# Weight-block sums made by accumulating DMAs instead of VectorE, in a seven-product matrix scheme with other signs

## The chip, the cores and the metric

The kernel runs on one core of one Trainium2 chip. The metric is the device time of one execution in microseconds, as the median of several runs. The kernel before took 1541.83 us (median of three, 1540.9 to 1542.78).

## The reference

Two layers of an encoder over 512 positions of width 2048, all in float32. Each layer normalises its input, multiplies it by one wide weight (`w_in`, 2048 x 4928), feeds three groups of heads and a gate, and projects back with `w_o` (2048 x 2048):

```python
for l in range(DEPTH):
    h = rmsnorm(x, pre_norm_g[l])
    z = h @ w_in[l]
    q_lat, kv_lat, k_pe, gb, gc, xin, q_mem, gate = split_cols(z)
    ...   # latent attention (8 heads), short gated convolution, attention over 256 memory tokens
    y = jnp.concatenate([a_out, c_out, m_out], axis=-1) * jax.nn.silu(gate)
    o = y @ w_o[l]
    x = x + rmsnorm(o, post_norm_g[l])
```

Only the two large products, `h @ w_in` and `y @ w_o`, are touched by the change.

## The kernel before, in words

**Precision.** A float32 operand is held as two parts that TensorE takes in one pass, `hi` and `lo`. A product is three matmuls, hi·hi, hi·lo and lo·hi (`mm3`, lines 233 to 235). A weight tile is split after it has been loaded: ScalarE makes `wh` (line 161), VectorE then makes `wl` as the difference (line 162).

**Seven products for eight.** The large products are worked out in groups of 1024 output columns (one group has 832). There are seven groups in a layer, five of `w_in` and two of `w_o`, so 14 in all. A group is a 2 x 2 block product, done by a scheme of the Strassen-Winograd kind: seven block products P1 to P7 on sums of blocks instead of eight. The left sums (`S1` to `S4`) are made once for a matrix by `combine` and split. The right sums are sums of weight blocks and are made for each group: T1 = B12 - B11, T2 = B22 - T1, T4 = B21 - T2 and T3 = B22 - B12. Before the change VectorE makes them out of loaded tiles (`sub`, line 408) into tiles of a pool `tf` (3 buffers), and they are split from there.

**Units and steps.** The depth of 1024 of a block is cut into four chunks, c = 0 to 3. A unit is one chunk of one block or sum, a tile of 128 x 1024 floats (512 KB). A step takes one unit and does 12 matmuls of 512 columns on it (2 row tiles, 2 halves of the chunk, 3 parts). `HEAD`, `STEADY`, `SECOND` and `LATE` list the passes of a group; a pass of several products takes their chunks in turn. `Program.run` walks the steps: before a step it issues loads some units ahead on the queue of SyncE (line 136, pool `raw`, 5 buffers) and emits the splits of units up to two steps ahead (`wh` and `wl` have three buffers each). Work that can wait (left sums, normalisation) is put in a queue and taken out as room allows.

**Order.** The instructions of TensorE and SyncE stand in the order in which the program records them; the others are put in order by a scheduler. VectorE has the splits, the sums, the evictions from PSUM and the softmax. GpSimd (POOL) has little: a few statistics of one column and some DMAs that are not weights.

Of the kernel before, what the change touches and what calls it, by code (L numbers as in the profile page):

```python
# [60 lines left out]
RAW, TF, PIECES, SLABS = 5, 3, 4, 19  # L61


class Unit:
# [4 lines left out]
    def __init__(self, loads, make=None, alloc=None, gain=None, split=True):  # L69
        self.loads = loads  # L70
        self.make = make
        self.alloc = alloc
        self.gain = gain
        self.split = split


class Program:
    def __init__(self, nc, raw, hi, lo, ahead=2, loads_ahead=3):
        self.nc = nc
        self.pools = raw, hi, lo  # L80
        self.ahead, self.loads_ahead = ahead, loads_ahead
        self.steps = []
        self.early = 0
        self.queue = []
# [29 lines left out]
    def run(self):  # L114
# [4 lines left out]
        at = {"load": 0, "prep": 0}  # L119

        def load(upto):
            upto = max(upto, self.early)
            while at["load"] < min(upto, len(seq)):
                for key, srcs in seq[at["load"]].loads:
                    if key in tiles:
                        continue
                    t = raw.tile([P, 1024], F32, tag="raw", name=f"wr{len(tiles)}")
                    off = 0
                    for src in srcs:
                        n = 1  # L130
                        for d in src.shape[1:]:
                            n *= d
                        dst = t[:, off:off + n]
                        if len(src.shape) == 3:
                            dst = dst.rearrange("p (a b) -> p a b", b=src.shape[2])
                        nc.sync.dma_start(dst, src)
                        off += n
                    tiles[key] = t[:, :off]
                at["load"] += 1

        self.load = load

        def prep(upto):
            while at["prep"] < min(upto, len(seq)):
                c = at["prep"]
                load(c + 1)
                u = seq[c]
                got = [tiles[key] for key, _ in u.loads]
                src = u.make(*got) if u.make else got[0]
                at["prep"] += 1  # L150
                if not u.split:
                    outs[c] = None
                    continue
# [15 lines left out]
                outs[c] = (hi[:, :n], lo[:, :n])  # L169

# [17 lines left out]
def encoder(tc, x, mem, positions, pre_norm_g, w_in, q_norm_g, w_uq, kv_norm_g, w_ukv, conv_w,  # L188
# [13 lines left out]
    tf_p = pool("tf", bufs=TF, reuse_waits="tile")  # L202
# [172 lines left out]
    def combine(left, p, a11, a12, a21, a22):  # L375

        def sub(out, a, b, op=ALU.subtract):
            pr.defer(1.2, lambda: nc.vector.tensor_tensor(out, a, b, op=op))

        def split(name, src):  # L380
            pr.defer(1.2, lambda: left.split(name, p, src))

        sub(a22, a21, a22, ALU.add)
        split("S1", a22)
        sub(a22, a22, a11)
        split("S2", a22)
        sub(a12, a12, a22)
        split("S4", a12)
        sub(a21, a11, a21)
        split("S3", a21)  # L390

    HEAD = [["P1"], ["P2"], ["P5", "P6", "P4"], ["P3", "P7"]]
    STEADY = [["P1", "P5", "P6", "P4"], ["P2"], ["P3", "P7"]]
    SECOND = [["P2"], ["P1"], ["P5", "P6", "P4"], ["P3", "P7"]]
    LATE = [["P2"], ["P3", "P1", "T3", "T1"], ["P6"], ["P5", "T4"], ["P7"], ["P4"]]

    def group(left, key, w, block, slot, passes, final, hold=None, by_two=False):
# [3 lines left out]
        bk, held, n = {}, {}, 2 * w  # L401
        late = passes is LATE

        def sub(name, c, a, b, dst=None):
            t = dst
            if t is None:
                t = tf_p.tile([P, 1024], F32, tag="tf", name=nm(name))[:, :n]
            nc.vector.tensor_tensor(t, a, b, op=ALU.subtract)  # L408
            held[name, c] = t
            return t  # L410

        def keep(name, c):
            if c % 2 == 0:
                held[name] = slab(name)
            return held[name][:, (c % 2) * 1024:(c % 2) * 1024 + n]

        def unit(q, c, k):
            def ld(h, j, again=False):
                return (key, k + 1 if again else 0, h, j, c), [block(h, j, c)]
            if q == "P1":  # L420
                return Unit([ld(0, 0, late or len(passes[k]) == 1)])
            if q == "P2":
                return Unit([ld(1, 0, True)])
            if q == "P3":
                return Unit([ld(1, 1, True)])
            if late:
                return {
                    "T1": lambda: Unit([ld(0, 1, True), ld(0, 0, True)],
                                       lambda a, b: sub("T1", c, a, b, keep("T1", c)), split=False),
                    "T3": lambda: Unit([ld(1, 1, True), ld(0, 1, True)],  # L430
                                       lambda a, b: sub("T3", c, a, b, keep("T3", c)), split=False),
                    "P6": lambda: Unit([ld(1, 1)], lambda a: sub("T2", c, a, held["T1", c], keep("T2", c))),
                    "P5": lambda: Unit([], lambda: held["T1", c]),
                    "T4": lambda: Unit([ld(1, 0)], lambda a: sub("T4", c, a, held["T2", c], held["T2", c]), split=False),
                    "P7": lambda: Unit([], lambda: held["T3", c]),
                    "P4": lambda: Unit([], lambda: held["T4", c], alloc=hold),
                }[q]()
            if q == "P5":
                return Unit([ld(0, 1), ld(0, 0)], lambda a, b: sub("T1", c, a, b))
            if q == "P6":  # L440
                return Unit([ld(1, 1)], lambda a: sub("T2", c, a, held["T1", c]))
            if q == "P4":
                return Unit([ld(1, 0)], lambda a: sub("T4", c, a, held["T2", c]))
            return Unit([ld(1, 1, True), ld(0, 1, True)], lambda a, b: sub("T3", c, a, b))
# [3 lines left out]
        def done(q, tt):  # L448
            ps = bk[q][tt][:, :w]
            s = {(i, j): slot(i, j, tt) for i in range(2) for j in range(2)}  # L450
            if q == "P2" and "P1" not in bk:
                nc.scalar.copy(s[0, 0], ps)
            elif q == "P1":
                nc.scalar.copy(s[1, 0], ps)
                if "P2" in bk:
                    plus(s[0, 0], s[0, 0], ps)
                    final(0, 0, tt)
            elif q == "P2":
                if bk["P2"] is bk["P1"]:
                    nc.scalar.copy(s[0, 0], ps)  # L460
                else:
                    plus(s[0, 0], s[1, 0], ps)
                final(0, 0, tt)
            elif q == "P6":
                plus(s[1, 0], s[1, 0], ps)
                plus(s[1, 1], s[1, 0], bk["P5"][tt][:, :w])
            elif q == "P4":
                plus(s[1, 0], s[1, 0], ps)
            elif q == "P3":
                plus(s[0, 1], s[1, 1], ps)  # L470
                final(0, 1, tt)
            elif q == "P7":
                plus(s[1, 1], s[1, 1], ps)
                final(1, 1, tt)
                plus(s[1, 0], s[1, 0], ps)
                final(1, 0, tt)

        def done_late(q, tt):
            ps = bk[q][tt][:, :w]
            s = {(i, j): slot(i, j, tt) for i in range(2) for j in range(2)}  # L480
            if q == "P2":
                nc.scalar.copy(s[0, 0], ps)
            elif q == "P3":
                nc.scalar.copy(s[0, 1], ps)
            elif q == "P1":
                plus(s[0, 0], s[0, 0], ps)
                final(0, 0, tt)
            elif q == "P6":
                nc.scalar.copy(s[1, 0], ps)
            elif q == "P5":  # L490
                plus(s[0, 1], s[0, 1], ps)
                nc.scalar.copy(s[1, 1], ps)
                final(0, 1, tt)
            elif q == "P7":
                plus(s[1, 1], s[1, 1], ps)
                final(1, 1, tt)
                plus(s[1, 0], s[1, 0], ps)
# [4 lines left out]
        ended = done_late if late else done  # L502

        def products(q, c, tt, ops, chained):
            hi, lo = (a.rearrange("p (j c) -> p j c", j=2) for a in ops)
            pr.until(lambda: left.there(LEFT[q], 2 * c, tt))
            for j in range(2):
# [3 lines left out]
        def step(q, c, chained):  # L511
            def f(*ops):
                if q[0] == "T":
                    return
                if c == 0:
                    bk[q] = bk["P1"] if chained else [bank(q), bank(q)]
                for tt in range(2):
                    products(q, c, tt, ops[0], chained)
# [4 lines left out]
        def two(q, c):  # L523
            def f(*ops):
                bk[q] = [bank(q), bank(q)]
                for tt in range(2):
                    for d in range(2):
                        products(q, c + d, tt, ops[d], False)
            return f

        def whole(q):
            def f(*ops):
                bk[q] = [bank(q), bank(q)]
                for tt in range(2):
                    for c in range(4):
                        products(q, c, tt, ops[c], False)
# [3 lines left out]
        def rooms(q):  # L540
            if q in ("P1", "P2", "P3") or late and q in ("P5", "P7", "P4"):
                return 1.4
            return -1.2 if q[0] == "T" else 0.2

        out = []
        for k, names in enumerate(passes):
            if names == ["P4"] and hold:
                out.append([(whole("P4"), [unit("P4", c, k) for c in range(4)], 4.0)])
                continue
            chained = passes is STEADY and names == ["P2"] or late and names[0] in ("P6", "P5")  # L550
# [842 lines left out]
```

## Time and profile before

| | before |
|---|---|
| median of three runs | 1541.83 us |
| the profiled execution | 1541.63 us, span 1539.9 us, mean granted clock 0.99 |
| TensorE matmuls busy | 1500.9 us, 97% |
| VectorE busy | 1288.6 us, 84% |
| ScalarE busy | 857.7 us, 56% |
| GpSimd busy | 52.3 us, 3% |
| mean DMA rate | 179 GB/s |

Busy time is what the profiler counts per engine. Matmuls are pipelined, so a busy TensorE also holds time in which it only waits in its pipe. A DMA that an engine issues is not counted as busy on it. The table of DMA issues gives, for each kind of transfer, the queue and the median time from issue to landing.

### The profile page before, as it was taken

The page shows a single profiled execution, that of the slowest core. Times are in us where ns is not written, and L with a number is a line of the kernel's source. Part 1 is how long each engine was busy: PE and PEld are TensorE (multiplying, and loading weights), DVE is VectorE, ACT ScalarE, POOL GpSimd, SP SyncE. Part 2 cuts the span into 40 slices and gives each one's busy share as a digit, 9 for nine tenths or more (in the row PEclk, how much of TensorE's full clock was granted, in tenths as well). Part 3 has the DMA queues.
Part 4 walks back from the last instruction along what each step waited for, and adds up shares of the span by engine and source line. Part 5 has one row for each costly group of instructions (what it writes and reads, how often), then busy time and mean ns, then how long its engine had stood idle before and what let it go on. Part 6 is the DMA issues. An engine that isn't in the chain of part 4 may idle for free.

```text
span 1539.9 us, 20320 instructions
## 1 busy us (share of the span) xinstructions
PE 1500.9 (97%) x7613; PEld 1283.8 (83%) x7613; DVE 1288.6 (84%) x1642; ACT 857.7 (56%) x1323; POOL 52.3 (3%) x89
## 2 busy tenths in 40 slices
PE   9999999999999999998999999999999999999997
PEld 7788888988898888886888888888988888887775
DVE  6999979797967668898788989979798586789987
ACT  7643443455567768644588533443454587775433
POOL 1000000010000000000220000000010000000001
PEclk9999999999999999999999999999999999999998
DMA  7577565666581112466967776565667410046573
GB/s 288 170 242 247 166 205 175 186 211 225 158 275 60 42 42 71 158 228 203 353 205 234 243 254 214 188 193 171 186 198 221 132 45 29 28 145 208 180 243 140
DMA packets 146934, 275.59 MB, mean 179 GB/s; under 512 B 17340, under 2 KB 40212, under 8 KB 143508
## 3 DMA queue, kind: packets, MB, share of 16 engines
q1 hardware_dynamic: 142032, 246.99, 49.9%
q0 software_dynamic: 4672, 27.27, 4.8%
q8 instruction: 59, 0.97, 0.3%
q14 instruction: 39, 0.32, 0.1%
q10 hardware_dynamic: 132, 0.05, 0.0%
HBM read 259.59 MB, written 14.68 MB: 178 GB/s over the span
## 4 chain that ended last, share of the span: by engine, by line
PE 72%; DVE 16%; ACT 5%; issue 4%; DMA 3%; POOL 1%; DVEq 0%; SPq 0%; POOLq 0%; ACTq 0%
PE P L234 16%; PE P L235 16%; PE P L233 16%; DVE wl L162 5%; DMA wr<-in_w_o_dram 3%; DVE T L408 2%; PE ptp L996 2%; ACT wh L161 1%; PE tps L754 1%; DVE og L446 1%; PE sc L233 1%; PE o L234 1%; PE sc L234 1%; PE sc L235 1%; PE o L233 1%
## 5 line engine op out<-in xcount | busy, mean ns | idle before, releaser
L161 ACT CAST wh<-T 128x1024 fp32r<-128x1024 f32 (+1 forms) x220 | 226.3, 1029 | 314.4 <-PE P L235 203.4
L234 PE MATMUL P<-wl,S 128*128 128x512 f32 (+1 forms) x896 | 348.3, 389 | 12.8 <-DVE wl L162 12.8
L233 PE MATMUL P<-wh,S 128*128 128x512 f32 (+1 forms) x896 | 348.7, 389 | 1.3 <-ACT wh L161 1.3
L235 PE MATMUL P<-wh,S 128*128 128x512 f32 (+1 forms) x896 | 346.5, 387 | 0.2 <-DVE S L239 0.2
L162 DVE TENSOR_TENSOR wl<-T,wh 128x1024 fp32r<-128x1024 f32 (+1 forms) x220 | 261.6, 1190 | 52.0 <-ACT wh L161 51.1
L161 ACT CAST wh<-wr 128x1024 fp32r<-128x1024 f32 (+1 forms) x188 | 194.5, 1037 | 176.8 <-PE P L235 146.2
L162 DVE TENSOR_TENSOR wl<-wr,wh 128x1024 fp32r<-128x1024 f32 (+1 forms) x188 | 224.0, 1194 | 58.8 <-ACT wh L161 57.8
L234 PE MATMUL P<-wl,A 128*128 128x512 f32 (+1 forms) x656 | 252.6, 385 | 2.7 <-DVE wl L162 2.7
L233 PE MATMUL P<-wh,A 128*128 128x512 f32 (+1 forms) x656 | 254.0, 387 | 1.1 <-ACT wh L161 1.0
L235 PE MATMUL P<-wh,A 128*128 128x512 f32 (+1 forms) x656 | 252.5, 385 | 0.5 <-DVE A L239 0.5
L234 PEld LDWEIGHTS P<-wl,S 128*128 128x128 f32 x896 | 170.0, 190 | 47.0 <-DVE wl L162 17.4
L233 PEld LDWEIGHTS P<-wh,S 128*128 128x128 f32 x896 | 169.8, 190 | 32.1 <-ACT wh L161 2.1
L235 PEld LDWEIGHTS P<-wh,S 128*128 128x128 f32 x896 | 170.0, 190 | 31.5 <-DVE S L239 0.6
L408 DVE TENSOR_TENSOR T<-wr,wr 128x1024 f32<-128x1024 f32 (+1 forms) x112 | 132.5, 1190 | 20.5 <-DMA wr<-in_w_in_dram 14.2
L234 PEld LDWEIGHTS P<-wl,A 128*128 128x128 f32 x656 | 123.7, 189 | 25.4 <-DVE wl L162 3.7
L233 PEld LDWEIGHTS P<-wh,A 128*128 128x128 f32 x656 | 123.7, 189 | 23.7 <-ACT wh L161 1.9
L235 PEld LDWEIGHTS P<-wh,A 128*128 128x128 f32 x656 | 123.4, 188 | 23.5 <-DVE A L239 1.2
L408 DVE TENSOR_TENSOR T<-wr,T 128x1024 f32<-128x1024 f32 (+1 forms) x112 | 132.9, 1191 | 6.4 <-DMA wr<-in_w_o_dram 3.2
L982 ACT ACTIVATE P<-sc,nm 128x512 f32<-128x512 f32 (+1 forms) x96 | 60.2, 629 | 35.2 <-DVE nm L979 34.6
L985 ACT ACTIVATE P<-P,rec 128x512 f32<-128x512 f32 (+1 forms) x96 | 62.5, 665 | 6.3 <-DVE rec L984 6.3
L979 DVE TENSOR_REDUCE nm<-sc 128x1 f32<-128x512 f32 (+1 forms) x96 | 56.8, 594 | 8.3 <-PE sc L977 6.0
L239 DVE TENSOR_TENSOR PT<-ptp,PT 128x512 fp32r<-128x512 f32 (+1 forms) x96 | 56.5, 593 | 4.7 <-ACT PT L238 4.5
(256 smaller groups left out, 2278.4 us busy)
## 6 DMA issues: line engine op xcount, KB each, us to landing
wr<-in_w_in_dram SPq DMA_DIRECT2D x240, 512.0 KB, 4.7
wr<-in_w_o_dram SPq DMA_DIRECT2D x112, 512.0 KB, 4.7
wr<-in_w_in_dram SPq DMA_DIRECT2D x56, 416.0 KB, 3.9
wr<-in_w_mk_dram SPq DMA_DIRECT2D x16, 512.0 KB, 3.9
wr<-in_w_mv_dram SPq DMA_DIRECT2D x16, 512.0 KB, 4.3
wr<-in_w_uq_dram SPq DMA_DIRECT2D x24, 256.0 KB, 3.4
x<-in_x_dram SPq DMA_DIRECT2D x4, 1024.0 KB, 7.7
wr<-in_w_ukv_dram SPq DMA_DIRECT2D x8, 512.0 KB, 3.8
```

The source lines that it names most:

```text
L161: nc.scalar.copy(hi[:, :n], src)
L162: nc.vector.tensor_tensor(lo[:, :n], src, hi[:, :n].bitcast(F32), op=ALU.subtract)
L233: nc.tensor.matmul(ps, ah, bh, start=first, stop=False, **kw)
L234: nc.tensor.matmul(ps, ah, bl, start=False, stop=False, **kw)
L235: nc.tensor.matmul(ps, al, bh, start=False, stop=last, **kw)
L239: nc.vector.tensor_tensor(lo, src, hi.bitcast(F32), op=ALU.subtract)
L408: nc.vector.tensor_tensor(t, a, b, op=ALU.subtract)
L446: plus = lambda o, a, b: nc.vector.tensor_tensor(o, a, b, op=ALU.add)
L979: nc.vector.tensor_reduce(nmax, ps, axis=AX.X, op=ALU.max, negate=True)
L982: nc.scalar.activation(pt, ps, AF.Exp, bias=nmax, accum_out=tot)
L985: nc.scalar.activation(pt, pt, AF.Copy, scale=rec)
L996: nc.tensor.transpose(ps[:, k * P:(k + 1) * P], pt[:, k * P:(k + 1) * P], G["ident"])
```

## The change

The scheme uses other signs, so that a right sum is got from the one before by adding a block: with T starting as B11, T + B12, then + B22, then + B21 serve P5, P6 and P4 in turn; B22 + B12 serves P7, after B22 itself has served P3. The tile stays where it was loaded. Each addition is a DMA that GpSimd issues, which reads the block from memory and adds it to the tile in place (`accum_op=ALU.add`). It may start when both parts of the tile's split have been made, and the next split of the tile waits until it has landed. `sub` and the pool `tf` go; `raw` has 8 buffers instead of 5, and loads are issued up to 6 units ahead of the splits instead of 3.

The passes are in another order, the same for both groups of `w_o` (`LATE` goes). P1, P6 and P4 add up in one PSUM bank (in the two `HEAD` groups of a layer P6 and P4 alone). GpSimd's instructions now stand in the recorded order too. The evictions change signs and places, and their number stays near what it was.

```diff
-RAW, TF, PIECES, SLABS = 5, 3, 4, 19
+RAW, PIECES, SLABS = 8, 4, 19
...
+        users = {}
+        for c, u in enumerate(seq):
+            users.setdefault(u.key, []).append(c)
+        after = {a: b for cs in users.values() for a, b in zip(cs, cs[1:])}
+        first_more = [c for c, u in enumerate(seq) if u.more is not None and users[u.key][0] == c]
...
+        def more(c):
+            u = seq[c]
+            move(nc.gpsimd, tiles[u.key], 0, u.more, accum_op=ALU.add)
...
             while at["prep"] < min(upto, len(seq)):
                 c = at["prep"]
                 load(c + 1)
+                while first_more and first_more[0] <= c + self.more_ahead:
+                    load(first_more[0] + 1)
+                    more(first_more.pop(0))
                 u = seq[c]
-                got = [tiles[key] for key, _ in u.loads]
-                src = u.make(*got) if u.make else got[0]
+                src = tiles[u.key]
...
                 outs[c] = (hi[:, :n], lo[:, :n])
+                if c in after:
+                    more(after[c])
...
-    HEAD = [["P1"], ["P2"], ["P5", "P6", "P4"], ["P3", "P7"]]
-    STEADY = [["P1", "P5", "P6", "P4"], ["P2"], ["P3", "P7"]]
-    SECOND = [["P2"], ["P1"], ["P5", "P6", "P4"], ["P3", "P7"]]
-    LATE = [["P2"], ["P3", "P1", "T3", "T1"], ["P6"], ["P5", "T4"], ["P7"], ["P4"]]
+    HEAD = [["P1"], ["P2"], ["P5"], ["P6", "P3"], ["P7"], ["P4"]]
+    STEADY = [["P1"], ["P5", "P2"], ["P6", "P3"], ["P7"], ["P4"]]
+    SECOND = [["P2"], ["P1"], ["P5"], ["P6", "P3"], ["P7"], ["P4"]]
...
             if q == "P1":
+                return of("P1" if apart else "T", (0, 0))
             if q == "P5":
+                return of("T", *([(0, 0)] if apart else []), more=(0, 1))
+            return {"P6": lambda: of("T", more=(1, 1)), "P4": lambda: of("T", more=(1, 0), alloc=hold),
+                    "P2": lambda: of("P2", (1, 0)), "P3": lambda: of("B22", (1, 1)),
+                    "P7": lambda: of("B22", more=(0, 1))}[q]()
...
-    with tc.manual_schedule(engines={mybir.EngineType.PE, mybir.EngineType.SP}):
+    with tc.manual_schedule(engines={mybir.EngineType.PE, mybir.EngineType.SP, mybir.EngineType.Pool}):
         pr.run()
```

How the order of instructions moves shows at two places. The first is GpSimd (POOL) in the projection of the first layer. Before, between the statistics of the last rows of x (`r_331`) and those of the latents (`ms_2868`) it has nothing; all five groups of `w_in` lie between the two:

```order
L245 TENSOR_TENSOR r_331<-ms_329,mhalf 128x1
L243 TENSOR_SCALAR ms_2868<-ssq_209_2863 128x4
```

In the changed kernel the accumulating DMAs stand there, 16 to a group. This is the pass of P6 and P3 in the third group (`wr_1322` to `wr_1378` are the four tiles of T, the others the four of B22), and the first two of the next group; a row ends with the semaphores waited for (`DMASW` an earlier DMA of GpSimd, `DMAHW` one of SyncE, `DVE` VectorE):

```order
L134 DMA wr_1322<-in_w_in_dram 128x2x512 [waits DMASW4_49,DVE_49]
L134 DMA wr_1572<-in_w_in_dram 128x2x512 [waits DMAHW7_49,DMAHW3_49,DVE_49]
L134 DMA wr_1342<-in_w_in_dram 128x2x512 [waits DMASW5_49,DVE_49]
L134 DMA wr_1624<-in_w_in_dram 128x2x512 [waits DMAHW4_49,DMAHW0_49,DVE_49]
L134 DMA wr_1360<-in_w_in_dram 128x2x512 [waits DMASW6_49,DVE_49]
L134 DMA wr_1673<-in_w_in_dram 128x2x512 [waits DMAHW5_49,DMAHW1_49,DVE_49]
L134 DMA wr_1378<-in_w_in_dram 128x2x512 [waits DMASW7_49,DVE_49]
L134 DMA wr_1724<-in_w_in_dram 128x2x512 [waits DMAHW6_49,DMAHW2_49,DVE_49]
L134 DMA wr_1899<-in_w_in_dram 128x2x416 [waits DMASW1_49,DMAHW3_49,DMASW0_49,DVE_49]
L134 DMA wr_1919<-in_w_in_dram 128x2x416 [waits DMAHW4_49,DMASW3_49,DVE_49]
```

An addition for P4 (to T) and one for P7 (to B22) alternate, all eight within the pass of P6 and P3, and none stands in the passes of P7 and P4. In all 224 loads leave SyncE's queue for GpSimd's.

The second place is VectorE in the fourth group of the first layer (832 columns). Before, nearly every split (L162) has a sum of blocks (L408) beside it:

```order
L408 TENSOR_TENSOR T_173_2268<-wr_2202,wr_2176 128x832
L162 TENSOR_TENSOR wl_2229<-T_168_2226,wh_2228 128x832
L408 TENSOR_TENSOR T_176_2290<-wr_2224,T_173_2268 128x832
L162 TENSOR_TENSOR wl_2249<-wr_2176,wh_2248 128x832
L408 TENSOR_TENSOR T_177_2310<-wr_2246,T_176_2290 128x832
```

In the changed kernel the splits stand alone, straight from the loaded tiles:

```order
L173 TENSOR_TENSOR wl_2090<-wr_1899,wh_2089 128x832
L173 TENSOR_TENSOR wl_2109<-wr_1993,wh_2108 128x832
L173 TENSOR_TENSOR wl_2127<-wr_1919,wh_2126 128x832
L173 TENSOR_TENSOR wl_2148<-wr_2028,wh_2147 128x832
L173 TENSOR_TENSOR wl_2166<-wr_1937,wh_2165 128x832
```

The 224 sums are gone from VectorE, and each split of a sum now reads a tile that a DMA of GpSimd wrote last.

More of the change, by code (lines that the diff above doesn't have):

```diff
@@ L547, in group @@
             if names == ["P4"] and hold:
-                out.append([(whole("P4"), [unit("P4", c, k) for c in range(4)], 4.0)])
+                out.append([(whole("P4"), [unit("P4", c) for c in range(4)], 4.0)])
                 continue
-            chained = passes is STEADY and names == ["P2"] or late and names[0] in ("P6", "P5")
-            steps = [(step(q, c, chained), [unit(q, c, k)], rooms(q)) for c in range(4) for q in names]
+            steps = [(step(q, c), [unit(q, c)], room(q, c)) for c in range(4) for q in names]
             if names == ["P7"] and hold:
@@ L554, in group @@
             if by_two and k == 0:
-                steps[:2] = [(two(names[0], 0), [unit(names[0], c, k) for c in range(2)], 0.0, 1)]
+                steps[:2] = [(two(names[0], 0), [unit(names[0], c) for c in range(2)], 0.0, 1)]
             out.append(steps)
@@ L857, in unit @@
         def unit(kp):
[L858 removed]
+            return Unit(("qr", l, kp), [wl[:, 2 * kp + a, :, NOPE:] for a in range(2)])
         def products(kp):
```

235 lines of the change are left out of this document (96 added, 139 removed).

## The prediction

> **What bounds the kernel now.** I read the page's busy times and chain first, then TensorE stage by stage, then what the weak stages wait for.
>
> ```profile
> span 1539.9 us, 20320 instructions
> PE 1500.9 (97%) x7613; PEld 1283.8 (83%) x7613; DVE 1288.6 (84%) x1642; ACT 857.7 (56%) x1323; POOL 52.3 (3%) x89
> PE 72%; DVE 16%; ACT 5%; issue 4%; DMA 3%; POOL 1%; DVEq 0%; SPq 0%; POOLq 0%; ACTq 0%
> ```
>
> TensorE is the bound: 97% busy, and 72% of the chain. VectorE is second, with 16% of the chain. The pace of a step comes from the timeline of TensorE: 36 matmuls lie between the starts of these two.
>
> ```profile
> 59.30 0.39 PE L233 MATMUL P<-wh,A 128*128 128x512 f32 x1
> ...
> 67.46 0.39 PE L233 MATMUL P<-wh,A 128*128 128x512 f32 x1
> ```
>
> 8.16 / 36 = 0.2267 us each, so a step of 12 takes 2.72 us and a group of 28 steps 76.2 us. Where TensorE falls behind, the windows of 20 us tell (columns: window, its length, then busy time and count of PE, PEld, DVE, ACT, POOL, then PE clock, DMA share, GB/s):
>
> ```profile
> 40.00:60.00 20.00, 18.01 (x72) 14.11 (x71) 17.99 (x18) 14.86 (x28) 0.00 (x0) 0.91 0.48 152
> 60.00:80.00 20.00, 18.21 (x79) 14.55 (x78) 20.00 (x20) 9.87 (x10) 0.00 (x0) 1.00 0.67 228
> 640.00:660.00 20.00, 18.96 (x84) 15.40 (x83) 19.97 (x20) 13.64 (x17) 0.00 (x0) 1.00 0.40 133
> 660.00:680.00 20.00, 20.00 (x90) 16.57 (x89) 19.86 (x20) 7.38 (x7) 0.00 (x0) 1.00 0.76 258
> 700.00:720.00 20.00, 17.89 (x72) 14.36 (x71) 18.15 (x23) 9.26 (x18) 0.00 (x0) 0.91 0.51 168
> 720.00:740.00 20.00, 16.72 (x61) 13.04 (x60) 17.42 (x17) 8.29 (x12) 0.85 (x2) 0.83 0.90 313
> 1400.00:1420.00 20.00, 18.96 (x84) 15.37 (x83) 20.00 (x20) 11.63 (x15) 0.00 (x0) 1.00 0.61 201
> 1460.00:1480.00 20.00, 17.85 (x72) 14.25 (x72) 17.20 (x18) 6.91 (x11) 0.00 (x0) 0.91 0.54 174
> 1480.00:1500.00 20.00, 17.12 (x68) 13.48 (x67) 18.55 (x19) 10.16 (x14) 2.13 (x4) 0.91 0.76 266
> ```
>
> The window from 660 is a full one, 90 matmuls. The other eight miss 18, 11, 6, 18, 29, 6, 18 and 22, in all 128. At 0.2267 us that is **29 us**, the clock that drops after a pause included. VectorE is full or nearly so in most of them, and what TensorE waits for there is its split or a load:
>
> ```profile
> PE P L234 <- DVE wl L162: 15.5, 13, 2.4
> ...
> 718.97 6.88 DMA wr<-in_w_o_dram
> ```
>
> (The first is a row of the waits: total, times, longest; the second a piece of the chain, start and length.) So a perfect supply of operands is worth 29 us. The rest of the span is matmuls, the start and the end, which the change leaves.
>
> **What the change removes.** The groups of costliest work show the sums and the splits:
>
> ```profile
> L408 DVE TENSOR_TENSOR T<-wr,wr 128x1024 f32<-128x1024 f32 (+1 forms) x112 | 132.5, 1190 | 20.5 <-DMA wr<-in_w_in_dram 14.2
> L408 DVE TENSOR_TENSOR T<-wr,T 128x1024 f32<-128x1024 f32 (+1 forms) x112 | 132.9, 1191 | 6.4 <-DMA wr<-in_w_o_dram 3.2
> L161 ACT CAST wh<-wr 128x1024 fp32r<-128x1024 f32 (+1 forms) x188 | 194.5, 1037 | 176.8 <-PE P L235 146.2
> L162 DVE TENSOR_TENSOR wl<-wr,wh 128x1024 fp32r<-128x1024 f32 (+1 forms) x188 | 224.0, 1194 | 58.8 <-ACT wh L161 57.8
> ```
>
> VectorE loses 132.5 + 132.9 = 265 us, a fifth of its work. Since it is not the bound, this pays only the 29 us above, and I credit all of them: no stage is left in which it would be full.
>
> **What it adds.** 224 accumulating DMAs, each between two splits of the same tile. The shortest distance is from P1 to P5, and from P7's last addition to its split: four steps, 10.9 us. Nothing in the trace is such a DMA. What bounds it (issue, queue, count, size, median time to landing; and the two queues):
>
> ```profile
> q1 hardware_dynamic: 142032, 246.99, 49.9%
> q0 software_dynamic: 4672, 27.27, 4.8%
> wr<-in_w_in_dram SPq DMA_DIRECT2D x240, 512.0 KB, 4.7
> xs<-xr POOLq DMA_DIRECT2D x8, 512.0 KB, 3.7
> Kmd<-Km POOLq DMA_DIRECT2D x1, 1024.0 KB, 5.7
> Vm<-Vmd POOLq DMA_DIRECT2D x1, 1024.0 KB, 6.2
> ```
>
> An accumulation writes 512 KB and reads 1 MB, 512 KB of it from the tile. GpSimd's plain 512 KB take 3.7 us, its single megabytes 5.7 and 6.2 us. I call its time X and take the middle between 3.7 and 6.2, **X = 4.95 us**; both ends stay in the range.
>
> Whether X matters depends on whether the next accumulation may be on its way while one is. Plain DMAs of GpSimd may:
>
> ```profile
> 1497.17 1.13 POOL L1148 DMA_DIRECT2D xr<-xs  x2 [4.91 <-PE P L235]
> ```
>
> Two are issued within 1.13 us here, long before the first can have landed. But those have one row of 8 KB for each of 128 partitions; q0's 4672 packets for 27.27 MB average 5.8 KB. An accumulation has two rows of 2 KB in each partition, and each is read twice, four times the rows to describe, in the same 1024 bytes a partition that the kernel gives GpSimd's DMAs (`dynamic_dma_scratch_size`, line 1381, unchanged). I take it that there is room for one at a time. This is the choice on which the forecast rests, and no row shows it.
>
> The Trainium skill would have it so, as an estimate: by "DMA: Bandwidth & Descriptors" (sections "Terms", "The descriptor swizzle" and "SWDGE vs HWDGE vs iDMA") a descriptor has 16 bytes, a side's ring lies in 16 partitions, and an engine gets one descriptor per row and one to complete; by "Collectives: The Full Stack" (Part 3) an add takes two read descriptors. That is 64 places for an engine's reads, and 2 x 16 + 1 = 33 for one accumulation, so two do not fit. No run here shows it yet.
>
> **The sum.** With one at a time, a group cannot be faster than its 16 X and the stretch in which none is under way. That stretch runs from the landing of P7's last addition to the first split of the next group, after which the next addition may go. It holds the split of P7's last unit (1.04 + 1.19 = 2.23 us), three steps (with three buffers of `wh`, the split of P1's first chunk waits for the second step of P4; 8.16 us) and that split (2.23 us): 12.6 us. GpSimd takes its DMAs in order, so the eight of the pass of P6 and P3 stand in one line though P4's are needed last; P7's wait behind them, and behind a late P7 wait its split, TensorE and the next group.
>
> - 14 groups: 14 x (16 x 4.95 + 12.6) = 1109 + 177 = 1286 us.
> - TensorE's own pace there: 5 groups of 28 steps and 2 of 24 in a layer (P2 of the `w_o` groups is done in the attention), 376 x 2.72 = 1023 us.
> - Loss 263 us, gain 29 us, so 1541.6 - 29 + 263 = **1776 us** against the profiled execution's own 1541.63, which lies 0.2 us under the median.
>
> It begins to decide at X = (1023 - 177) / 224 = 3.8 us. At 4.2 us the same sum gives 1608, at 6.2 us 2056.
>
> **Edits taken at nothing.** The evictions from PSUM change signs and places, not their number to speak of, and the 265 us freed on VectorE cover them. SyncE's queue loses 224 loads and only gets lighter. GpSimd's statistics of the latents now stand behind an addition and in front of others; they wait up to X twice, under a group's steps. In a long wait the clock may drop as it did from 720 (0.83); of the 12.6 us that would stretch three steps by 1.4 us, at most 20 us in all, inside the range.
>
> **Rivals.**
>
> *Hidden additions* (the other side): GpSimd has several under way, or one takes under 3.8 us. Then each has its 10.9 us and more, TensorE never waits for one, and only the gain is left: 1541.6 - 29 = 1513 us. For it: the two issues within 1.13 us, and 3.7 us for plain 512 KB. Against: the second read, and the room for rows. It ends once an addition takes over 3.8 us alone, or over some 7.5 us with two under way. A rule of the Trainium skill speaks for it: "DMA: Bandwidth & Descriptors", section "Anatomy of one DMA — SWDGE (gpsimd) path", gives 2.0 us and the bytes at 436 GB/s, for 512 KB an estimate of 3.2 us, by which the sum is this rival's 1513 us. The trace has 3.7 us for the plain transfer.
>
> *The DMA engines fill up*: the additions overlap, but each costs two reads. By q1, 246.99 MB took 49.9% of 1539.9 us, so 1.63 us of all engines for 512 KB. A group then needs 16 x 3.26 + 12 x 1.63 = 71.7 of its 76.2 us. At a share of 0.90, as from 720, loads were already late. 71.7 / 0.9 = 79.7, 3.5 us more in each of 14 groups: 1513 + 49 = 1562 us.
>
> *Nothing gained, nothing lost*: the additions hide, but the stalls stay with the left sums and loads of the same stages: 1541 us. Against it: VectorE is full in those stages, and in its order nearly every second instruction is a sum that goes.
>
> **How the numbers follow.** One at a time 0.66, with its own range of 1608 to 2056 us; hidden 0.22; engines full 0.07; nothing 0.05. A difference within 0.2% (3 us) is what a measurement here cannot tell from none. Faster is the second case, 0.22; the same is the last, 0.05; slower are the first and third, 0.73. The time is that of the likeliest, 1776 us. The range takes in the second and third cases and the likeliest up to X = 6.2: 1510 to 2055 us, with less than 2 in 10 outside.
>
> **What will show it.** Right, if TensorE's waits name VectorE's or ScalarE's split behind a DMA `wr` of GpSimd, worst in P7 and in the first chunks of P5; if GpSimd's issues follow one another at one distance of 4 to 6 us through the pass of P6 and P3; if VectorE's busy time is near 1020 us at the same time. Wrong, if several additions are under way at once, if TensorE stays at 97%, or if the stages from 40, 700 and 1460 us keep their gaps though the additions landed early.

## The result, and the profile after

The changed kernel takes **2099.15 us** (median of 2094.4 to 2099.56), the kernel before 1542.3 us beside it (1540.9 to 1543.94): a ratio of 1.3603, interval 1.3579 to 1.3627. The prediction said slower, 1776 us, within 1510 to 2055. The direction and the cause held; the time lies 323 us above the predicted one and 44 us above the range.

From the page of the changed kernel (busy times; the queues; the shares of the chain; one row of the costliest groups; the DMA issues with the median time to landing):

```profile
span 2097.4 us, 20239 instructions
PE 1665.4 (79%) x7613; PEld 1362.3 (65%) x7613; DVE 1038.0 (49%) x1398; ACT 856.4 (41%) x1335; POOL 314.3 (15%) x313
...
q0 software_dynamic: 65600, 141.57, 37.6%
q1 hardware_dynamic: 81104, 132.68, 19.5%
...
issue 55%; PE 24%; POOL 11%; DMA 4%; DVE 3%; ACT 3%; POOLq 0%; DVEq 0%; ACTq 0%
...
L134 POOL DMA_DIRECT2D wr<-in_w_in_dram x160 | 194.5, 1216 | 904.2 <-issue 632.9
...
wr<-in_w_in_dram POOLq DMA_DIRECT2D x128, 512.0 KB, 5.7
```

TensorE has fallen from 97% to 79%, and from 72% of the chain to 24%. No engine and no queue is full. VectorE lost 1288.6 - 1038.0 = 251 us, and nothing became of it. What leads the chain is "issue", time in which an engine waits for nothing that the profile shows, and the engine is GpSimd: it is busy for 15% of the span and idle before its additions, 632.9 us of it without a releaser. (The text on the profile before says that an issued DMA is not counted as busy. For GpSimd it is: the 224 issues of 1.2 us each are 272 of its 314.3 us.) Its timeline at the end of the second group of the first layer (start, length, and in brackets the idle time before it) shows how such a limit looks:

```profile
200.07 1.22 POOL L134 DMA_DIRECT2D wr<-in_w_in_dram  x1 [4.86 <-issue]
206.14 1.21 POOL L134 DMA_DIRECT2D wr<-in_w_in_dram  x1 [4.85 <-issue]
212.05 1.22 POOL L134 DMA_DIRECT2D wr<-in_w_in_dram  x1 [4.70 <-issue]
...
236.26 1.21 POOL L134 DMA_DIRECT2D wr<-in_w_in_dram  x1 [4.69 <-issue]
256.51 1.21 POOL L134 DMA_DIRECT2D wr<-in_w_in_dram  x1 [19.04 <-DVE wl L173]
```

Six distances from 200.07 to 236.26 make 6.03 us each, against 5.7 us from issue to landing: the next one goes some 0.3 us after the last has landed. Then comes 20.25 us in which the next group's first addition waits for VectorE. The waits (total, times, longest) name the same places from the other side:

```profile
POOL wr L134 <- issue: 857.2, 175, 7.6
ACT wh L172 <- DMA wr<-in_w_in_dram: 577.7, 85, 11.2
PE P L245 <- ACT wh L172: 320.4, 65, 6.9
ACT wh L172 <- DMA wr<-in_w_o_dram: 245.0, 37, 11.4
PE P L246 <- DVE wl L173: 72.0, 84, 15.4
```

GpSimd waits 175 times for something unnamed, ScalarE's split waits for GpSimd's DMA, TensorE for the split. Taken one by one in the trace, all 122 of ScalarE's waits for a `wr`, 823 us, end with the landing of an addition: 572 us with one of P7's, 165 with one of P6's, 85 with one of P5's and none with one of P4's. The prediction had named P7 and the first chunks of P5; in P5 it is the later chunks that wait, and P6 it had not named. That the unnamed thing is the room for descriptors has to be shown by experiments.

### The profile page after: what moved, and what is told of

Read it like the earlier page. It is cut to its first block, busy times and chain, and to the rows that moved or that the text cites. A ratio compares the mean times of both kernels' runs of the same rounds, so it can differ in the third digit from the quotient of the medians.

```text
span 2097.4 us, 20239 instructions
## 1 busy us (share of the span) xinstructions
PE 1665.4 (79%) x7613; PEld 1362.3 (65%) x7613; DVE 1038.0 (49%) x1398; ACT 856.4 (41%) x1335; POOL 314.3 (15%) x313
## 3 DMA queue, kind: packets, MB, share of 16 engines
q0 software_dynamic: 65600, 141.57, 37.6%
## 4 chain that ended last, share of the span: by engine, by line
issue 55%; PE 24%; POOL 11%; DMA 4%; DVE 3%; ACT 3%; POOLq 0%; DVEq 0%; ACTq 0%
POOL wr L134 10%; PE P L246 2%; PE P L247 2%; PE P L245 2%; DMA wr<-in_w_in_dram 2%; PE ptp L973 1%; DMA wr<-in_w_o_dram 1%; DVE wl L173 1%; PE o L246 1%; DMA mL<-mTd 1%; PE sc L245 1%; PE sc L246 1%; PE sc L247 1%; PE o L247 1%; PE o L245 1%
## 5 line engine op out<-in xcount | busy, mean ns | idle before, releaser
L173 DVE TENSOR_TENSOR wl<-wr,wh 128x1024 fp32r<-128x1024 f32 (+1 forms) x408 | 482.0, 1195 | 883.9 <-ACT wh L172 883.0
L172 ACT CAST wh<-wr 128x1024 fp32r<-128x1024 f32 (+1 forms) x408 | 413.9, 1030 | 1077.3 <-DMA wr<-in_w_in_dram 577.7
L245 PE MATMUL P<-wh,S 128*128 128x512 f32 (+1 forms) x896 | 407.4, 455 | 320.5 <-ACT wh L172 320.4
L246 PE MATMUL P<-wl,S 128*128 128x512 f32 (+1 forms) x896 | 405.4, 452 | 71.5 <-DVE wl L173 71.2
L245 PEld LDWEIGHTS P<-wh,S 128*128 128x128 f32 x896 | 198.3, 221 | 390.0 <-ACT wh L172 353.0
L247 PE MATMUL P<-wh,S 128*128 128x512 f32 (+1 forms) x896 | 388.8, 434 | 0.0
L134 POOL DMA_DIRECT2D wr<-in_w_in_dram x160 | 194.5, 1216 | 904.2 <-issue 632.9
L246 PEld LDWEIGHTS P<-wl,S 128*128 128x128 f32 x896 | 197.8, 221 | 145.6 <-DVE wl L173 109.4
L247 PEld LDWEIGHTS P<-wh,S 128*128 128x128 f32 x896 | 198.8, 222 | 36.3
L134 POOL DMA_DIRECT2D wr<-in_w_o_dram x64 | 77.8, 1215 | 689.9 <-DVE rec L961 362.6
L178 DVE SCALAR_TENSOR_TENSOR wl<-wr,cols,wh 128x512 fp32r<-128x512 f32 x64 | 46.3, 747 | 14.1 <-ACT wh L177 13.8
L177 ACT ACTIVATE wh<-wr,cols 128x512 fp32r<-128x512 f32 x64 | 44.1, 721 | 20.8 <-PE mv L247 7.6
```

Source lines behind the costliest of these rows:

```text
L134: engine.dma_start(dst, src, **kw)
L172: nc.scalar.copy(hi[:, :n], src)
L173: nc.vector.tensor_tensor(lo[:, :n], src, hi[:, :n].bitcast(F32), op=ALU.subtract)
L177: nc.scalar.activation(hi[:, h], src[:, h], AF.Copy, scale=g)
L178: nc.vector.scalar_tensor_tensor(lo[:, h], src[:, h], g, hi[:, h].bitcast(F32), op0=ALU.mult, op1=ALU.subtract)
L245: nc.tensor.matmul(ps, ah, bh, start=first, stop=False, **kw)
```

## The experiments

Eleven kernels ran. Theory A is the prediction's: the descriptor room lets one addition be under way at a time. Theory B: GpSimd, its queue or the order of its row takes them one by one whatever the room. Theory C: the DMA engines are the limit. All edits are to the changed kernel, but for the control.

| Kernel | us | ratio to before (interval) |
|---|---|---|
| the change, 1024 bytes of room | 2099.15 | 1.3603 (1.3579 to 1.3627) |
| 1088 bytes | 1600.49 | 1.0381 (1.0351 to 1.0411) |
| 1536 bytes | 1599.79 | 1.0382 (1.0353 to 1.0411) |
| 2048 bytes | 1529.87 | 0.9923 (0.9900 to 0.9947) |
| each addition in two halves, 1024 bytes | 1699.71 | 1.1025 (1.0993 to 1.1057) |
| plain copies, room for one | 1801.55 | one time |
| plain copies, 1024 bytes | 1526.8 | one time |
| no additions at all | 1525.37 | 0.9894 (0.9865 to 0.9922) |
| P4's additions after P7's, 1024 bytes | 2018.87 | 1.3100 (1.3056 to 1.3143) |
| P4's after P7's, 2048 bytes | 1564.55 | 1.0146 (1.0121 to 1.0170) |
| P5's and P4's sums on VectorE, 1024 bytes | 1662.64 | 1.0793 (1.0755 to 1.0831) |
| the kernel before with 2048 bytes | 1540.97 | 1.0001 (0.9987 to 1.0014) |

**64 bytes more.** The smallest edit that tells A from B:

```diff
-    nc = bacc.Bacc("TRN2", ..., dynamic_dma_scratch_size=1024)
+    nc = bacc.Bacc("TRN2", ..., dynamic_dma_scratch_size=1088)
```

> The changed kernel with one number altered: 1088 bytes a partition for GpSimd's descriptors instead of 1024. Theory A (one accumulation at a time for want of room: 33 of 64 places for one, an estimate from the Trainium skill; with 68 places two fit): the additions overlap in pairs, the distance between GpSimd's issues falls from 6.1 us to 3.0 to 4.0 us (3.2 us is what the 16 engines need for one by the queue's share, 37.6% of 2097 us less the 74 us of the plain ones, over 224), and the time falls to 1530 to 1620 us. Rival B (accumulations follow one another whatever the room, because each reads and writes its tile): distance stays at 6.1 us, time stays at 2099 us within 1%. Rival C (the 16 DMA engines are the bound): no more than a few per cent is won, 2000 us or more.

Measured: 1600.49 us, 499 us less. The page and the waits of this run:

```profile
PE 1522.1 (95%) x7613; PEld 1296.1 (81%) x7613; DVE 1040.5 (65%) x1398; ACT 862.2 (54%) x1335; POOL 315.1 (20%) x313
...
q0 software_dynamic: 65600, 141.57, 49.0%
```

```profile
POOL wr L134 <- DVE wl L173: 469.9, 118, 24.4
...
POOL wr L134 <- issue: 146.4, 70, 4.8
ACT wh L172 <- DMA wr<-in_w_in_dram: 76.1, 14, 8.8
```

GpSimd's unnamed wait fell from 857.2 to 146.4 us, and it now waits mostly for VectorE, as the program's order wants it. The median distance between its additions fell from 6.1 to 3.4 us. The work is the same to the packet (65600, 141.57 MB). B is out: nothing else was touched. But 1600 us is 75 above the kernel without additions (below), so something still limits. Of the 127 us that ScalarE still waits for additions (76.1 of `w_in`, 51.1 of `w_o`), 111 are for the last two of P7's in a group, which stand behind P4's in GpSimd's row.

**More room: 1536 and 2048 bytes.** One scratch tile that nothing reads was halved in type to make the space.

```diff
-        G.update(..., junk=const.tile([P, 512], F32, name="junk"))
+        G.update(..., junk=const.tile([P, 512], mybir.dt.bfloat16, name="junk"))
...
-    nc = bacc.Bacc("TRN2", ..., dynamic_dma_scratch_size=1024)
+    nc = bacc.Bacc("TRN2", ..., dynamic_dma_scratch_size=2048)
```

> Room for three additions under way (2048 bytes of descriptor room; an unread scratch tile was halved in type to fit). With room for two the time was 1600 us, the profile's accumulating queue took 49% of the DMA engines and all DMA slices but a few stood at 8 or 9 tenths. Theory C (with two under way the DMA engines are the bound): no more to be had, 1570 to 1610 us, and the distances stay at 3.2 to 3.4 us. Theory A (room is still the bound): distances fall to 2.1 to 2.5 us and the time to 1525 to 1550 us.

> 1536 bytes of descriptor room: by the estimate of 33 places of 16 bytes for one accumulation, two fit (66 of 96 places) and three do not (99). Theory A (room counts in whole accumulations): nothing is gained over 1088 bytes, 1585 to 1615 us. Rival (more room helps steadily): between the 1600 us of 1088 bytes and the 1530 us of 2048, about 1555 to 1570 us.

Measured: 1529.87 us with 2048 bytes, 1599.79 with 1536. The second is the run with 1088 again to within 1 us, with 448 bytes more; the first is 70 us faster. The room counts in whole additions: 1088 and 1536 behave alike, 2048 is the next step. By the Trainium skill ("DMA: Bandwidth & Descriptors", "Terms" and "The descriptor swizzle", and "Collectives: The Full Stack", Part 3) the prediction had estimated 33 places of 16 bytes for an addition; 33, 66 and 99 places are 528, 1056 and 1584 bytes, and the steps between 1024 and 1088 and between 1536 and 2048 agree with it.

How many are under way can be counted in the traces, which have the issue and the landing of each of the 224 additions. With 1024 bytes there is never more than one, with 1088 and with 1536 never more than two, with 2048 never more than three, and the most is reached in 224, 201, 203 and 148 of the 224 issues. With room for n, no addition is issued sooner than some 0.3 us after the n-th before it has landed. So by the runs alone an addition takes more than 512 bytes of room, as two don't fit in 1024, and at most 544, as two fit in 1088.

From the page of the run with 2048 bytes (span, TensorE, DMA busy tenths in 40 slices, queues), and its waits:

```profile
span 1528.1 us, 20239 instructions
PE 1493.4 (98%) x7613; PEld 1281.5 (84%) x7613; DVE 1039.8 (68%) x1398; ACT 864.6 (57%) x1335; POOL 315.4 (21%) x313
...
DMA  8999898989581112699997999897989411048895
...
q0 software_dynamic: 65600, 141.57, 48.6%
q1 hardware_dynamic: 81104, 132.68, 26.9%
```

```profile
POOL wr L134 <- issue: 38.7, 26, 5.0
...
ACT wh L172 <- DMA wr<-in_w_o_dram: 18.5, 9, 4.5
...
ACT wh L172 <- DMA wr<-in_w_in_dram: 11.9, 6, 2.9
```

TensorE is at 98%, and ScalarE waits 18.5 + 11.9 = 30 us for additions where it waited 823. Theory C, which I had taken as likely after the run with 1088 bytes because its DMA slices stood at 8 and 9 tenths, is refuted too: they stand at 8 and 9 tenths here, and nobody waits for them to speak of, though an addition takes 7.0 us to land with three under way and 5.7 with one.

This kernel beats the one before by 0.8%. So that the room itself isn't taken for the cause, the kernel before got the same two edits:

> The kernel before with the same 2048 bytes of room and the same scratch tile halved in type: a control for the version that beats it. Its own GpSimd DMAs (89 instructions on GpSimd in all) never wait for room, so 1538 to 1545 us. Rival (the room itself, and not the change, gave the 0.8%): 1525 to 1535 us.

Measured: 1540.97 us, ratio 1.0001. The room alone does nothing; the change with room is what gains.

**Halves.** Two additions of one row for each partition in place of one of two rows, in 1024 bytes:

```diff
-            move(nc.gpsimd, tiles[u.key], 0, u.more, accum_op=ALU.add)
+            off = 0
+            for a in range(2):
+                off = move(nc.gpsimd, tiles[u.key], off, u.more[:, a, :], accum_op=ALU.add)
```

> Room for descriptors as in the changed kernel (1024 bytes), but each addition is made by two accumulating DMAs of 128 rows instead of one of 256: the same bytes, half the descriptors in each. Theory A (room): three of them fit at a time, so transfers overlap; GpSimd's issue of 1.2 us for each, 2.4 us for a pair, and the engines' 3.2 us for a pair bound it, so about 3.5 us for a chunk and 1530 to 1650 us in all. Rival B (one after another whatever the room): two fixed parts of about 2.6 us each and two halves of the transfer, 2 x (2.6 + 1.75) = 8.7 us for a chunk in place of 6.1, so 224 x 2.6 = 580 us more, about 2680 us.

Measured: 1699.71 us, 50 above the upper end for A, and far from B's. From its waits:

```profile
POOL wr L134 <- issue: 347.4, 300, 5.5
```

By the same estimate a half needs 17 places, and three halves fit in 64: one and a half additions under way. The trace has three halves under way at 392 of the 448 issues, and never four. The time lies between one (2099) and two (1600). A's range had asked for as much overlap as two whole additions have, and that was the miss.

**Plain copies.** Are one-at-a-time and its price due to the adding? The sums are missing in both runs.

```diff
-            move(nc.gpsimd, tiles[u.key], 0, u.more, accum_op=ALU.add)
+            move(nc.gpsimd, tiles[u.key], 0, u.more)
...
-    nc = bacc.Bacc("TRN2", ..., dynamic_dma_scratch_size=1024)
+    nc = bacc.Bacc("TRN2", ..., dynamic_dma_scratch_size=320)
```

(The last two lines in the first run only.)

> The same transfers on the same queue as plain copies (the sum is left out: the block overwrites the tile), with 320 bytes a partition for descriptors, so that by theory A only one fits at a time (17 of 20 places). It prices the add itself. Theory A: issues at one distance of 3.9 to 4.5 us (6.1 less the second read, about 1.6 us by the engines' share for 512 KB), and by the prediction's sum with 4.2 us, 1513 + 224 x 4.2 + 177 - 1023 = 1608 us, 1580 to 1680 us. Rival B (the add is what holds up the queue, plain copies overlap): distance under 3 us where the splits allow it, TensorE never waits for them, 1510 to 1545 us.

> The 224 additions are made plain copies into the same tiles, so the sums are missing, and the room for descriptors stays 1024 bytes, which three plain copies fit into. With room for one plain copy the time was 1802 us at a distance of 4.4 us. Theory A (room decides how many are under way, and an addition costs the DMA engines twice a copy): two or three copies under way, distance under 2.7 us where nothing else holds them, 1520 to 1550 us. Theory B (GpSimd or its queue takes one DMA after the other whatever the room): 1780 to 1810 us.

Measured: 1801.55 us with room for one, 1526.8 with 1024 bytes. The first run's queue and landing, and the end of a group in its timeline; then the same of the second, with its issue row:

```profile
q0 software_dynamic: 35904, 141.57, 25.5%
...
wr<-in_w_in_dram POOLq DMA_DIRECT2D x128, 512.0 KB, 4.1
```

```profile
171.99 0.73 POOL L134 DMA_DIRECT2D wr<-in_w_in_dram  x1 [3.59 <-issue]
177.16 0.73 POOL L134 DMA_DIRECT2D wr<-in_w_in_dram  x1 [4.44 <-issue]
181.53 0.73 POOL L134 DMA_DIRECT2D wr<-in_w_in_dram  x1 [3.64 <-issue]
...
191.30 0.73 POOL L134 DMA_DIRECT2D wr<-in_w_in_dram  x1 [3.62 <-DVE gb L621]
212.39 0.73 POOL L134 DMA_DIRECT2D wr<-in_w_in_dram  x1 [20.37 <-DVE wl L173]
```

```profile
q0 software_dynamic: 35904, 141.57, 30.2%
...
L134 POOL DMA_DIRECT2D wr<-in_w_in_dram x160 | 115.8, 724 | 557.2 <-DVE wl L173 452.0
...
wr<-in_w_in_dram POOLq DMA_DIRECT2D x128, 512.0 KB, 4.6
```

Plain copies go one by one too when the room is small: 4.4 to 5.4 us apart, (191.30 - 171.99) / 4 = 4.8 in the mean, with a landing of 4.1, and never two under way in the whole trace. So it is the room, not the adding, that puts them in a row. The adding lengthens a place in that row, from 4.8 to 6.2 us in the mean of all distances inside the groups, and takes more room: 1024 bytes hold three copies (the most under way in the second run) and one addition. The time that I expected for the first (1580 to 1680) was 120 us too low: the copies lie 4.8 us apart where I had taken 4.2, and the passage to the next group's first copy took 21.1 us here. With these two the sum makes 14 x (15 x 4.8 + 21.1) = 1303 us, less 1023 a loss of 280, and on top of the 1525 us of the run without additions 1805. That it comes so near is in part luck, since only eight of the passages in the trace are of this kind. With room for three the copies cost as good as nothing, and no wait is left unnamed.

**No additions.** What is the gain worth with supply perfect? The additions are left out, and so the sums are missing:

```diff
         def more(c):
             u = seq[c]
-            move(nc.gpsimd, tiles[u.key], 0, u.more, accum_op=ALU.add)
+            return
```

> The changed kernel with the 224 additions left out (tiles are used as loaded, so the sums are missing from the result). It prices what the change takes off VectorE alone. The prediction's 29 us: all stalls in the eight windows vanish, 1513 us, 1505 to 1525. Rival: the stalls lie in the left sums and loads, 1535 to 1545 us.

Measured: 1525.37 us, 1.06% under the kernel before: 16 us, where the prediction had 29. Windows of 20 us (columns as in the prediction) tell where the rest went; first the kernel before at its end, then the run without additions:

```profile
1500.00:1520.00 20.00, 19.82 (x88) 16.09 (x87) 16.60 (x18) 10.66 (x15) 5.28 (x4) 1.00 0.34 139
1520.00:1540.00 20.00, 9.88 (x44) 7.85 (x42) 12.78 (x19) 2.90 (x8) 1.48 (x4) 0.80 0.40 158
```

```profile
40.00:60.00 20.00, 19.04 (x83) 15.23 (x82) 19.30 (x18) 16.53 (x30) 0.00 (x0) 1.00 0.56 170
740.00:760.00 20.00, 17.21 (x75) 13.48 (x73) 14.43 (x18) 12.62 (x20) 7.24 (x13) 1.00 1.00 384
1480.00:1500.00 20.00, 14.40 (x62) 11.21 (x60) 12.26 (x17) 8.03 (x14) 4.62 (x8) 0.91 0.52 198
1500.00:1520.00 20.00, 12.54 (x47) 9.58 (x47) 14.75 (x18) 4.01 (x9) 1.48 (x4) 0.84 0.53 207
```

From 1460 to its end at 1539.9 us the kernel before has 72 + 68 + 88 + 44 = 272 matmuls, 80 fewer than those 79.9 us hold. Without additions there are 62 + 47 = 109 from 1480 to the end at 1522.8, again 80 fewer. The 18 and 22 that I had counted from 1460 and 1480 came back as a longer wait at the very end. At the first layer's end 15 are missing from 740 instead of 18 + 29 from 700, and 7 are still missing from 40. Of 128, 128 - 40 - 15 - 7 = 66 were gained, 15 us.

**The order in GpSimd's row.** P4's four additions of a group after P7's:

```diff
-        users = {}
+        users, late = {}, []
...
                 if c in after:
-                    more(after[c])
+                    b = after[c]
+                    if seq[b].key[1] == "T" and b == users[seq[b].key][-1]:
+                        late.append(b)
+                    else:
+                        more(b)
+                        while seq[b].key[1:] == ("B22", 3) and late:
+                            more(late.pop(0))
```

> P4's four additions of a group are issued after P7's instead of ahead of them; everything else as in the change. Theory A (one addition under way, and the head of GpSimd's row waits for VectorE at the group's turn): the distance inside a run of additions stays at 6.1 us, and only the dead stretch of about 20 us in each group shrinks, to 6 to 12 us; 14 groups make 110 to 200 us, so 1900 to 1990 us. Theory B (the order in GpSimd's row is of no account, the groups are paced by the 16 additions and TensorE's work alone): 2080 to 2115 us.

> Both mendings together: 2048 bytes of room and P4's additions issued after P7's. If P7's wait behind P4's is what is left between 1530 us (2048 bytes) and 1525 us (no sums at all): 1524 to 1528 us. If three under way already hide it, or P4's additions are now the late ones: 1528 to 1540 us.

Measured: 2018.87 us with 1024 bytes, 80 us less than the change; 1564.55 us with 2048 bytes, 35 us more than with the order of the change. The turn of a group in the first of these, and the waits of the second:

```profile
348.46 1.22 POOL L134 DMA_DIRECT2D wr<-in_w_in_dram  x1 [4.89 <-issue]
358.10 1.22 POOL L134 DMA_DIRECT2D wr<-in_w_in_dram  x1 [8.42 <-DVE wl L173]
```

```profile
ACT wh L172 <- DMA wr<-in_w_in_dram: 99.8, 40, 3.7
POOL wr L134 <- issue: 93.7, 33, 4.3
...
ACT wh L172 <- DMA wr<-in_w_o_dram: 41.0, 18, 3.4
```

With one at a time the long distance at the turn fell from 20.25 to 9.64 us, as expected; the distances inside a run are 6.2 us, and the time came out 29 us above the range that I gave, which had counted 10 us and more for every group. Only eight of the 13 passages from one group to the next have such a turn: they make 160.8 us together in the change and 79.6 here, 81 us less, and the kernel gained 80. With room for three it goes the other way: ScalarE waits 141 us for additions against 30, and 90 us of them are for the last four in a group's row, which are P4's. An order that is right under one limit is wrong under the next.

**Half of the sums back on VectorE.** An attempt to beat both kernels with the room as it is: P5's and P4's second blocks come by SyncE's queue and are added on VectorE, so only 8 additions are left in a group.

```diff
...
+                if on_dve(u):
+                    t = raw.tile([P, 1024], F32, tag="raw", name=f"wx{at['load']}")
+                    beside[at["load"]] = t[:, :move(nc.sync, t, 0, u.more)]
...
+                if on_dve(u):
+                    nc.vector.tensor_tensor(src, src, beside.pop(c), op=ALU.add)
...
-                if c in after:
+                if c in after and not on_dve(seq[after[c]]):
```

> P5's and P4's second blocks come through SP's queue as plain loads and are added by VectorE in place (as many sums on VectorE as that makes, 8 of 16 in a group); only P6's and P7's are accumulating DMAs, 8 in a group. Theory A: 8 x 6.2 = 50 us lie inside a group's 75 us of matmuls, VectorE has room for 8 x 1.2 us more, and the saved matmuls are seen: 1515 to 1535 us, about 1% below the kernel before. Rival: the additions of P6 and P7 stand in runs of four with their blocks due at 2.7 us each, so each run still holds TensorE back by about 4 x (6.2 - 2.7) = 14 us less what is loaded ahead: 1560 to 1750 us.

Measured: 1662.64 us; the rival was right. From its page and the timeline of GpSimd:

```profile
PE 1549.3 (93%) x7613; PEld 1300.7 (78%) x7613; DVE 1155.9 (70%) x1510; ACT 860.9 (52%) x1335; POOL 188.8 (11%) x201
```

```profile
334.37 1.21 POOL L137 DMA_DIRECT2D wr<-in_w_in_dram  x1 [4.78 <-issue]
364.06 1.21 POOL L137 DMA_DIRECT2D wr<-in_w_in_dram  x1 [28.48 <-DVE wl L181]
```

By the average, 8 x 6 = 48 us had to hide in a group's 76. But all eight fall into the part between P5 of one group and P7 of the same, and from the last of them to the first of the next 29.7 us go by in which GpSimd waits for VectorE. Seven distances of some 6.2 and one of 29.7 make 73 us at the least, and the distances are longer where a split is late. ScalarE waits 290 us for DMAs here, all of them for these eight additions of a group, and 25 us for VectorE's sums. What the second blocks cost by taking buffers of `raw`, which still has eight, was not measured apart.

## Why the prediction was wrong, point by point

- **One at a time, for want of room**: right, and the choice on which the forecast rested. 1024, 1088, 1536 and 2048 bytes gave 2099, 1600, 1600 and 1530 us.
- **X = 4.95 us**: the step that failed, by its size. I took the middle of 3.7 and 6.2 us; the landing took 5.7 and the distance from one issue to the next 6.0 to 6.2, at the upper bound. Two things were mis-sized. The plain copy of two rows of 2 KB in each partition already takes 4.8 us from issue to issue (4.1 to landing). The 3.7 us that I had for it is of transfers the other way, from the tile to memory, in rows of 4 KB; which of these differences made them shorter no run separates. And the adding costs 1.4 us more. Besides, X had to be a distance between issues, some 0.3 us longer than the landing that I took from the rows. With 6.1, 14 x 16 x (6.1 - 4.95) = 258 of the 323 us are accounted for, and the sum would give 2034 us, still inside the range; the other 65 us are in the next three points.
- **The gain of 29 us**: 16 us measured. Of the missing matmuls I had credited all; those at the two layers' ends were followed by other waits that came in their place. That is 13 us more.
- **The turn-around of 12.6 us**: a little too short, 20.25 - 6.1 = 14.1 us in the group shown, and counted too often. I took all 14 groups to have one. Of the 13 passages from one group to the next, eight are 18.8 to 20.9 us long. The two from the first to the second group of a layer are 6.1 and 6.0 us: there T is loaded apart from P1's block, so its first addition waits for no split. The other three hold the attention or the passage to the next layer. Eight times 14.0 us make 112 us, where the sum had 177. The clock explains part of the length: over the turn shown it was granted at 0.82.

```profile
236.00:256.50 20.50, 14.17 (x54) 10.83 (x53) 9.65 (x10) 7.18 (x9) 1.21 (x1) 0.82 0.62 174
```

- **The sum**: with the three measured sizes it gives 1541.6 - 16 + 14 x (16 x 6.1 + 14.1) - 1023 = 2066 us. That it comes within 33 us is luck. With the eight turns of the trace it gives 1541.6 - 16 + 224 x 6.1 + 112 - 1023 = 1981 us, so 118 us of the time are in none of its terms. The distances inside the groups are 6.23 us in the mean, not 6.1, which makes 28 of them. The other 90 are an overlap that the sum had wrong: it takes off all 1023 us of TensorE's work as if additions were under way beside all of it. In the trace some 410 of these 376 x 12 = 4512 matmuls, 93 us at 0.2267, run before a projection's first addition is issued or after its last has landed. With both the sum is 2102 us, 3 above the measured time. So six turns too many and this overlap had hidden each other. The mean clock was 0.879 against 0.990 before.
- **P4's additions ahead of P7's**: right under this limit, 80 us; wrong as a fault of the order in itself, since with room for three the same order is the better one by 35 us.
- **Edits at nothing**: TensorE's waits name splits and additions, and the runs without additions and with 2048 bytes came out below the kernel before, so the evictions, SyncE's loads and the statistics cost nothing that shows. The 265 us of sums were taken off VectorE nearly in full, 251.
- **Hidden additions** (0.22) is what happens once the room is there, 1530 us; its 1513 had the gain too large. Its condition "over some 7.5 us with two under way" was wrong: two under way at 6.1 us alone still left 75 us. It is an average over a group, and P7's last two additions were still late behind P4's (111 of the 127 us of ScalarE's waits for additions). The rule of the Trainium skill behind it ("DMA: Bandwidth & Descriptors", "Anatomy of one DMA — SWDGE (gpsimd) path"), 2.0 us and the bytes at 436 GB/s, an estimate of 3.2 us, is below both measured landings: 4.1 us for a plain copy with nothing else of GpSimd under way, 5.7 for an addition.
- **The DMA engines fill up** (0.07): the price of 3.26 us of all engines was near: q0's 48.6% of 1528.1 us, less its 4.8% of 1539.9 before, makes 2.99 us for each of 224, of which 32 are of 416 KB, and by the bytes 3.07 for 512 KB. The consequence was wrong: at 9 tenths TensorE went on at 98%.
- **The range** ended at X = 6.2 with all else as computed. It left no margin above for the gain, which was smaller, and for the part of TensorE's work that has no addition beside it.

## What to carry to other kernels

When GpSimd's DMAs follow one another at one distance just longer than their landing and the profile calls the idle time between them "issue", look for the room for their descriptors before anything else; here 1 KB more in each partition turned 36% slower into 0.8% faster. Price a serial resource by the distance from one use to the next, not by the time of one, and look at where its uses lie in the stage, since the mean over a group hid 75 us with two under way and up to 137 us with half of the additions gone. A gain counted from stalls is good only as far as nothing else ends just behind them: at the ends of the layers the next wait took half of it.

## What the runs showed that I had not expected

- The step is sharp: 64 bytes of descriptor room, with no instruction changed, were worth 499 us, and the next 448 bytes nothing.
- GpSimd's own issue grows with what it has to describe: 0.72 us for a plain copy of two rows, 1.21 us for the same with the add. 224 such issues make 271 us of GpSimd's time, which cost nothing here.
- In the mean of the 224, an addition takes the DMA engines 1.7 times the copy: 2.99 us against (30.2% of 1525.0, less 4.8% of 1539.9) / 224 = 1.73 us.
- DMA engines at 8 and 9 tenths through most of the projection were no limit with three additions under way.
